# A row-wise skewness kernel: written instruction order, a new cut of the late units, one last DVE step, and load semaphores seen ahead of the store

## The chip, the cores and the metric

The kernel runs on one core of a Trainium2 chip. The metric is device time in microseconds (us) of the slowest core, here the only one; medians over several runs. The span in a profile is about 1.8 us shorter than the device time, since it runs from the first instruction to the last.

## The reference

```python
# x: 1024 x 8192 float32
mean = np.mean(x, axis=-1, keepdims=True)
std  = np.std(x, axis=-1, keepdims=True)
z = (x - mean) / (std + 1e-8)
return np.mean(z ** 3, axis=-1).astype(np.float32)
```

The kernel needs three sums per row, of x, of x squared and of x cubed, and a little arithmetic on them. The 1024 rows are eight blocks of 128, and one block is cut into units along its 8192 columns.

## The kernel before

For each unit: one load; a square with a row sum on ACT (ScalarE); a cube with a row sum on DVE (VectorE), which multiplies the square by x; and transposes on PE (TensorE), which add up the row sum of x in PSUM. At the end of a block ACT copies the transposed sums to SBUF and a matmul makes the mean. (SBUF and PSUM are the core's two on-chip memories.)

```python
UNITS = [
    [4096, 4096], [4096, 4096], [4096, 4096], [4096, 4096],
    [3584, 2304, 2304],
    [2304, 2304, 2048, 1536],
    [1664, 1792, 1920, 1664, 1152],
    [1024, 1024, 1152, 1280, 1408, 1152, 1152],
]
...
    for b, widths in enumerate(UNITS):
        for k, w in enumerate(widths):
            last_unit = b == L and k == len(widths) - 1
            nc.sync.dma_start(out=xt, in_=xv[b, :, c0 : c0 + w])
            for s, e in _slices(w):                  # at most 2304 columns each
                # sq: in SBUF; in PSUM for the last unit
                nc.scalar.activation(out=sq, in_=xt[:, s:e], func=AF.Square, scale=s_scale,
                                     accum_out=s2u[:, j : j + 1])
                nc.vector.scalar_tensor_tensor(out=cube, in0=sq, scalar=1.0, in1=xt[:, s:e],
                                     op0=ALU.mult, op1=ALU.mult, accum_out=s3u[:, j : j + 1])
            ...                                      # transposes of x, added up in tp
            if k > 0:
                next(pending, None); next(pending, None)   # steps of the block before
        nc.scalar.copy(out=tsb, in_=tp)
        nc.tensor.matmul(out=s1ps[:, b : b + 1], lhsT=tsb, rhs=onesn, start=True, stop=True)
        ...
    for _ in pending: pass                           # the last block's small ACT steps
    nc.gpsimd.tensor_tensor(out=rr, in0=var2, in1=expo[:, 0 : NB - F], op=ALU.pow)
    nc.vector.tensor_reduce(out=num, in_=..., axis=X_AXIS, op=ALU.add)
    nc.vector.tensor_tensor(out=skew[:, F:NB], in0=num, in1=rr, op=ALU.mult)
    nc.sync.dma_start(out=ov, in_=skew)
```

A scheduler puts the instructions of each engine in order. Eight unit buffers are in rotation, so SyncE issues a load when the unit eight before it has been used by ACT, PE and DVE.

Of the kernel before, what the change touches and what calls it, by code (L numbers as in the profile page):

```python
# [8 lines left out]
FP = mybir.dt.float32  # L9
AF = mybir.ActivationFunctionType  # L10
ALU = mybir.AluOpType
X_AXIS = mybir.AxisListType.X


UNITS = [
    [4096, 4096],
    [4096, 4096],
    [4096, 4096],
    [4096, 4096],
    [3584, 2304, 2304],  # L20
    [2304, 2304, 2048, 1536],
    [1664, 1792, 1920, 1664, 1152],
    [1024, 1024, 1152, 1280, 1408, 1152, 1152],
]
S1_ACT = {(0, 0): 1024, (1, 0): 1024, (2, 0): 1024}
SUB_MAX = 2304
X_BUFS = 8
SQ_BUFS = 4
EARLY = 6


def _slices(w):
    n = -(-w // SUB_MAX)
    step = -(-w // n // 128) * 128
    return [(s, min(s + step, w)) for s in range(0, w, step)]


@with_exitstack
def kernel(
    ctx: ExitStack,  # L40
    tc: tile.TileContext,
    x: bass.AP,
    out: bass.AP,
):
    nc = tc.nc
    P = nc.NUM_PARTITIONS
    R, C = x.shape
    NB = R // P
    L = NB - 1
    F = EARLY  # L50
    inv_n = 1.0 / float(C)
    s_scale = float(C) ** -0.5
    third = (1.0 / 3.0) ** 0.5
    assert len(UNITS) == NB and all(sum(u) == C for u in UNITS)
    nw = len(S1_ACT)
    assert sorted(b for b, _ in S1_ACT) == list(range(nw)) and nw <= F


    xv = x.rearrange("(p b) c -> b p c", b=NB)
    ov = out.rearrange("(p b) -> p b", b=NB)  # L60


    K = max(sum(len(_slices(w)) for w in u) for u in UNITS) + 1

    xpool = ctx.enter_context(tc.tile_pool(name="xp", bufs=X_BUFS))
    sqpool = ctx.enter_context(tc.tile_pool(name="sqp", bufs=SQ_BUFS))
    onep = ctx.enter_context(tc.tile_pool(name="onep", bufs=1))
    psum = ctx.enter_context(tc.tile_pool(name="ps", bufs=2, space=bass.MemoryType.PSUM))
    psum1 = ctx.enter_context(tc.tile_pool(name="ps1", bufs=1, space=bass.MemoryType.PSUM))

    def small(name, n):
        return onep.tile([P, n], FP, tag=name, name=name)

    onesn = small("onesn", 1)
    nc.vector.memset(onesn, inv_n)  # L75
    tiny = small("tiny", 1)
    nc.scalar.activation(out=tiny, in_=onesn, func=AF.Square)  # L77
    ident = small("ident", P)
    make_identity(nc, ident)
    s2u = small("s2u", NB * K)  # L80
    s3u = small("s3u", NB * K)
    nc.vector.memset(s2u, 0.0)
    nc.vector.memset(s3u, 0.0)
    s1a = small("s1a", nw)
    same = small("same", max(S1_ACT.values()))
    junk = small("junk", K)
    expo = small("expo", F)
    nc.gpsimd.memset(expo, -1.5)
    skew = small("skew", NB)
    s1ps = psum1.tile([P, NB], FP, tag="s1ps")  # L90
    m1a = small("m1a", F)
    var2 = small("var2", NB - F)
    Tsb = [small(f"tsb{i}", P) for i in range(2)]

    def close_first_blocks():

        m2, m3 = small("m2a", F), small("m3a", F)
        for dst, src in ((m2, s2u), (m3, s3u)):
            nc.vector.tensor_reduce(  # L99
                out=dst, in_=src[:, 0 : F * K].rearrange("p (b c) -> p b c", c=K),  # L100
                axis=X_AXIS, op=ALU.add,
            )
        m1sq, m1sq3, nm1 = small("m1sqa", F), small("m1sq3a", F), small("nm1a", F)
        nc.scalar.copy(out=m1a[:, nw:F], in_=s1ps[:, nw:F])
        nc.scalar.activation(out=m1sq, in_=m1a, func=AF.Square)
        nc.scalar.activation(out=m1sq3, in_=m1a, func=AF.Square, scale=third)
        nc.scalar.activation(out=nm1, in_=m1a, func=AF.Copy, scale=-3.0)
        g = nc.gpsimd
        var, rr = small("vara", F), small("rra", F)
        g.tensor_tensor(out=var, in0=m2, in1=m1sq, op=ALU.subtract)  # L110
        g.tensor_tensor(out=m1sq3, in0=m1sq3, in1=var, op=ALU.add)  # L111
        g.tensor_tensor(out=m1sq3, in0=m1sq3, in1=nm1, op=ALU.mult)  # L112
        g.tensor_tensor(out=m3, in0=m3, in1=m1sq3, op=ALU.add)  # L113
        g.tensor_tensor(out=rr, in0=var, in1=expo, op=ALU.pow)  # L114
        g.tensor_tensor(out=skew[:, 0:F], in0=m3, in1=rr, op=ALU.mult)  # L115

    def close_on_act(b):

        m2, m1sq, nm1, v3 = (small(f"{t}_{b}", 1) for t in ("m2", "m1sq", "nm1", "v3"))
        p1 = s1ps[:, b : b + 1]  # L120
        var = var2[:, b - F : b - F + 1]
        act = nc.scalar.activation
        yield act(out=junk, in_=s2u[:, b * K : b * K + K], func=AF.Copy, accum_out=m2)
        yield act(out=m1sq, in_=p1, func=AF.Square)  # L124
        yield act(out=var, in_=m1sq, func=AF.Identity, scale=-1.0, bias=m2)  # L125
        yield act(out=nm1, in_=p1, func=AF.Copy, scale=-3.0)  # L126
        yield act(out=v3, in_=m1sq, func=AF.Identity, scale=1.0 / 3.0, bias=var)  # L127
        yield act(  # L128
            out=s3u[:, b * K + K - 1 : b * K + K], in_=v3, func=AF.Identity, scale=nm1
        )  # L130

    pending = iter(())
    for b, widths in enumerate(UNITS):
        tp = psum.tile([P, P], FP, tag="tp", name=f"tp_{b}")
        c0 = 0
        j = b * K
        for k, w in enumerate(widths):
            last_unit = b == L and k == len(widths) - 1
            xt = xpool.tile([P, w], FP, tag="x", name=f"x_{b}_{k}")
            nc.sync.dma_start(out=xt, in_=xv[b, :, c0 : c0 + w])  # L140
            c0 += w
            for s, e in _slices(w):
                if last_unit:
                    sq = psum1.tile([P, e - s], FP, tag="sqps", name=f"sqps_{s}")
                else:
                    sq = sqpool.tile([P, e - s], FP, tag="sq", name=f"sq_{b}_{k}_{s}")
                nc.scalar.activation(  # L147
                    out=sq, in_=xt[:, s:e], func=AF.Square, scale=s_scale,
                    accum_out=s2u[:, j : j + 1],
                )  # L150
                cube = sqpool.tile([P, e - s], FP, tag="sq", name="cube") if last_unit else sq
                nc.vector.scalar_tensor_tensor(  # L152
                    out=cube, in0=sq, scalar=1.0, in1=xt[:, s:e],
                    op0=ALU.mult, op1=ALU.mult, accum_out=s3u[:, j : j + 1],
                )
                j += 1
            w_act = S1_ACT.get((b, k), 0)
            if w_act:
                nc.scalar.activation(  # L159
                    out=same[:, 0:w_act], in_=xt[:, w - w_act : w], func=AF.Copy,  # L160
                    scale=inv_n, accum_out=s1a[:, b : b + 1],
                )
            n = (w - w_act) // P
            for c in range(n):
                nc.tensor.matmul(  # L165
                    out=tp, lhsT=xt[:, c * P : (c + 1) * P], rhs=ident,
                    start=(k == 0 and c == 0), stop=(c0 == C and c == n - 1),
                    is_transpose=True,
                )
            if k > 0:  # L170
                next(pending, None)
                next(pending, None)
        tsb = Tsb[b % 2]
        nc.scalar.copy(out=tsb, in_=tp)  # L174
        nc.tensor.matmul(out=s1ps[:, b : b + 1], lhsT=tsb, rhs=onesn, start=True, stop=True)  # L175
        if b == F - 2:
            nc.vector.tensor_tensor(
                out=m1a[:, 0:nw], in0=s1ps[:, 0:nw], in1=s1a, op=ALU.add
            )
        if b == F - 1:  # L180
            close_first_blocks()
        if b >= F:
            pending = close_on_act(b)
    for _ in pending:
        pass
    rr = small("rr2", NB - F)
    nc.gpsimd.tensor_tensor(out=rr, in0=var2, in1=expo[:, 0 : NB - F], op=ALU.pow)  # L187
    num = small("num2", NB - F)
    nc.vector.tensor_reduce(  # L189
        out=num, in_=s3u[:, F * K :].rearrange("p (b c) -> p b c", c=K), axis=X_AXIS, op=ALU.add  # L190
    )
    nc.vector.tensor_tensor(out=skew[:, F:NB], in0=num, in1=rr, op=ALU.mult)  # L192
    nc.sync.dma_start(out=ov, in_=skew)


# [28 lines left out]
```

## Time and profile before

| | before |
|---|---|
| median, us | 91.64 (91.61 to 91.72, three runs) |
| span of the profile, us | 89.7 |
| last load landed, us from the span's start | 83.56 |
| last DVE step starts | 87.04 |
| store issued / landed | 87.23 / 88.65 |
| DMA busy, share of the span | 90% |

Read the table from the end: of 89.7 us, 83.6 are the stream of loads, 3.5 the arithmetic after it, 1.6 the way to the landed store, and 1.1 the closing of the program. The busy shares of the engines tell why only the tail can be changed:

```profile
PE 64.9 (72%) x504; PEld 59.3 (66%) x504; DVE 72.7 (81%) x80; ACT 72.1 (80%) x106; POOL 11.3 (13%) x14
```

No engine is near the 90% of the loads. The other lines are in the prediction.

### The profile page before, as it was taken

What the parts mean: (1) busy time and instruction counts of PE and PEld (TensorE: products, weight loads), DVE (VectorE), ACT (ScalarE), POOL (GpSimd) and SP (SyncE); (2) the same over time, 40 slices, a digit from 0 to 9 for tenths busy, and PEclk for the clock granted to TensorE, in tenths of its full rate; (3) what the DMA queues carried; (4) which work ended last, traced back from release to release, by engine and by line L of the source; (5) the groups of instructions that cost most, each with busy time, mean ns of one, the idle gap of its engine ahead of it and who ended that gap; (6) DMA issues with size and microseconds to landing.
All of it is one profiled execution on the core that took longest, in us unless ns stands there. A gap on an engine that the chain in (4) does not pass through costs nothing.

```text
span 89.7 us, 1368 instructions
## 1 busy us (share of the span) xinstructions
PE 64.9 (72%) x504; PEld 59.3 (66%) x504; DVE 72.7 (81%) x80; ACT 72.1 (80%) x106; POOL 11.3 (13%) x14
## 2 busy tenths in 40 slices
PE   0003999892882919989998988888987798969710
PEld 0003999791872909979897977877876787848500
DVE  1000498989999298995999999999999999999970
ACT  6003999699991999859898989978979898999950
POOL 3000000000000000000000000000005999900030
PEclk9999999999999997599999999999999999999998
DMA  3999999999999999999999999999999999994000
GB/s 117 351 424 438 424 431 431 431 431 424 446 416 431 424 438 424 424 438 427 415 409 418 419 427 419 421 415 419 409 414 417 404 413 411 421 412 161 0 0 2
DMA packets 4038, 33.64 MB, mean 375 GB/s; under 512 B 576, under 2 KB 576, under 8 KB 2240
## 3 DMA queue, kind: packets, MB, share of 16 engines
q1 hardware_dynamic: 4032, 33.56, 89.7%
q8 instruction: 4, 0.07, 0.3%
q14 instruction: 2, 0.02, 0.0%
HBM read 33.55 MB, written 0.00 MB: 374 GB/s over the span
## 4 chain that ended last, share of the span: by engine, by line
DMA 73%; ACT 13%; issue 5%; DVE 4%; SPq 1%; PE 1%; DVEq 0%; ACTq 0%
DMA x<-in_x_dram 73%; ACT sq L147 9%; DVE sq L152 3%; ACT sqps L147 1%; ACT same L159 1%; SPq L140 1%; PE s1ps L175 1%; ACT tsb L174 0%; ACT s3u L128 0%; ACT v L127 0%; ACT var L125 0%; DVE num L189 0%; ACT m1sq L124 0%; DVE skew L192 0%; ACT nm L126 0%
## 5 line engine op out<-in xcount | busy, mean ns | idle before, releaser
L152 DVE SCALAR_TENSOR_TENSOR sq<-sq,x 128x2048 f32<-128x2048 f32 (+9 forms) x35 | 70.7, 2071 | 13.4 <-ACT sq L147 13.3
L165 PE MATMUL tp<-ident,x 128*128 128x128 f32 x488 | 62.6, 288 | 17.3 <-DMA x<-in_x_dram 17.2
L165 PEld LDWEIGHTS tp<-ident,x 128*128 128x128 f32 x488 | 57.9, 150 | 20.9 <-DMA x<-in_x_dram 12.7
L147 ACT ACTIVATE sq<-x 128x2048 f32<-128x2048 f32 (+9 forms) x35 | 60.6, 1734 | 10.7 <-DMA x<-in_x_dram 9.9
L110 POOL TENSOR_TENSOR vara<-m2a,m1sqa 128x6 f32<-128x6 f32 x1 | 1.8, 1822 | 67.1 <-DVE m3a L99 67.1
L147 ACT ACTIVATION_READ_ACCUMULATOR sq<-x 128x1 f32 x35 | 6.5, 186 | 0.0
L175 PEld LDWEIGHTS s1ps<-onesn,tsb 128*128 128x128 f32 x16 | 2.4, 188 | 5.2 <-ACT tsb L174 5.2
L175 PE MATMUL s1ps<-onesn,tsb 128*128 128x1 f32 x16 | 3.1, 260 | 3.3 <-ACT tsb L174 3.3
L174 ACT COPY tsb<-tp 128x128 f32<-128x128 f32 x8 | 2.0, 256 | 2.0 <-PE tp L165 2.0
L114 POOL TENSOR_TENSOR rra<-vara,expo 128x6 f32<-128x6 f32 x1 | 3.3, 3267 | 0.0
L159 ACT ACTIVATE same<-x 128x1024 f32<-128x1024 f32 x3 | 3.1, 1041 | 0.0
L152 DVE DVE_READ_ACCUMULATOR sq<-sq,x 128x1 f32 x35 | 2.9, 83 | 0.0
L111 POOL TENSOR_TENSOR m1sq3a<-m1sq3a,vara 128x6 f32<-128x6 f32 x1 | 1.9, 1868 | 0.1
L77 ACT ACT_TABLE_LOAD x1 | 1.3, 1283 | 0.7 <-PEq L208 0.7
L187 POOL TENSOR_TENSOR rr<-var,expo 128x2 f32<-128x2 f32 x1 | 0.7, 702 | 7.7 <-ACT var L125 7.7
L152 DVE SCALAR_TENSOR_TENSOR cube<-sqps,x 128x1152 f32<-128x1152 f32 x1 | 1.4, 1350 | 0.0
L113 POOL TENSOR_TENSOR m3a<-m3a,m1sq3a 128x6 f32<-128x6 f32 x1 | 1.2, 1201 | 0.1
L147 ACT ACTIVATE sqps<-x 128x1152 f32<-128x1152 f32 x1 | 1.1, 1136 | 0.1
L115 POOL TENSOR_TENSOR skew<-m3a,rra 128x6 f32<-128x6 f32 x1 | 1.1, 1069 | 0.1
L124 ACT ACTIVATE m1sq<-s1ps 128x1 f32<-128x1 f32 x2 | 0.3, 171 | 0.5 <-PE s1ps L175 0.5
L75 DVE MEMSET onesn<- 128x1 f32 x1 | 0.1, 59 | 0.8 <-PEq L208 0.8
L112 POOL TENSOR_TENSOR m1sq3a<-m1sq3a,nm1a 128x6 f32<-128x6 f32 x1 | 0.7, 697 | 0.0
(28 smaller groups left out, 6.8 us busy)
## 6 DMA issues: line engine op xcount, KB each, us to landing
x<-in_x_dram SPq DMA_DIRECT2D x8, 2048.0 KB, 23.4
x<-in_x_dram SPq DMA_DIRECT2D x4, 1152.0 KB, 27.9
x<-in_x_dram SPq DMA_DIRECT2D x4, 576.0 KB, 8.6
x<-in_x_dram SPq DMA_DIRECT2D x1, 1792.0 KB, 33.0
x<-in_x_dram SPq DMA_DIRECT2D x2, 832.0 KB, 13.9
x<-in_x_dram SPq DMA_DIRECT2D x1, 1024.0 KB, 21.1
x<-in_x_dram SPq DMA_DIRECT2D x2, 512.0 KB, 10.0
x<-in_x_dram SPq DMA_DIRECT2D x1, 960.0 KB, 13.2
```

The lines of the kernel that those rows point to most:

```text
L77: nc.scalar.activation(out=tiny, in_=onesn, func=AF.Square)
L110: g.tensor_tensor(out=var, in0=m2, in1=m1sq, op=ALU.subtract)
L111: g.tensor_tensor(out=m1sq3, in0=m1sq3, in1=var, op=ALU.add)
L113: g.tensor_tensor(out=m3, in0=m3, in1=m1sq3, op=ALU.add)
L114: g.tensor_tensor(out=rr, in0=var, in1=expo, op=ALU.pow)
L115: g.tensor_tensor(out=skew[:, 0:F], in0=m3, in1=rr, op=ALU.mult)
L147: nc.scalar.activation(out=sq, in_=xt[:, s:e], func=AF.Square, scale=s_scale, accum_out=s2u[:, j : j + 1],)
L152: nc.vector.scalar_tensor_tensor(out=cube, in0=sq, scalar=1.0, in1=xt[:, s:e], op0=ALU.mult, op1=ALU.mult, accum_out=s3u[:, j : j + 1],)
L159: nc.scalar.activation(out=same[:, 0:w_act], in_=xt[:, w - w_act : w], func=AF.Copy, scale=inv_n, accum_out=s1a[:, b : b + 1],)
L165: nc.tensor.matmul(out=tp, lhsT=xt[:, c * P : (c + 1) * P], rhs=ident, start=(k == 0 and c == 0), stop=(c0 == C and c == n - 1), is_transp ...
L174: nc.scalar.copy(out=tsb, in_=tp)
L175: nc.tensor.matmul(out=s1ps[:, b : b + 1], lhsT=tsb, rhs=onesn, start=True, stop=True)
```

## The change

It intends to shorten what follows the last load: a narrower last unit, small steps moved out of the way, one DVE step at the end instead of two, and no waits behind the store that could be done ahead of it. These are waits for semaphores, the counters by which a load or an engine tells another that it is done; the last lines of the diff, called the early look below, make SyncE wait for the loads' semaphores before the store. The wide units of blocks 2 and 3 are also worked on in three slices instead of two. The diff, cut to its core:

```diff
-    [3584, 2304, 2304],
-    [2304, 2304, 2048, 1536],
-    [1664, 1792, 1920, 1664, 1152],
-    [1024, 1024, 1152, 1280, 1408, 1152, 1152],
+    [3072, 2944, 2176],
+    [2944, 2688, 2560],
+    [1664, 1536, 1664, 1792, 1536],
+    [1024, 1152, 768, 1024, 1024, 1280, 1024, 896],
...
+SUB_WIDE = 1408            # units of 3584 and more, from block 2 on, in three slices
...
+    ctx.enter_context(tc.manual_schedule(          # orders as written
+        engines={eng.PE, eng.Activation, eng.DVE, eng.Pool, eng.SP}))
...
+    for b in range(L):                             # copy and mean behind the next block's first unit
+        at(b + 1, 0, lambda b=b: copy_sums(b))
+        at(b + 1, 0, lambda b=b: mean(b))
...
+    at(L, 0, mid_sums)                             # block 6: two reductions on DVE,
+    at(L, 1, mid_power)                            # power on POOL,
+    at(L, 4, lambda: third_1(mid))                 # two small ACT steps
+    at(L, 5, lambda: third_2(mid))
...
-    nc.vector.tensor_reduce(out=num, in_=..., axis=X_AXIS, op=ALU.add)
-    nc.vector.tensor_tensor(out=skew[:, F:NB], in0=num, in1=rr, op=ALU.mult)
+    g.tensor_tensor(out=o["var"], in0=o["m2"], in1=o["m1sq"], op=ALU.subtract)
+    g.tensor_tensor(out=o["rr"], in0=o["var"], in1=expo[:, 0:1], op=ALU.pow)
+    act(out=o["nm1"], in_=p1, func=AF.Copy, scale=-3.0)
+    third_1(o)                                     # v3 = m2 - 2/3 m1sq
+    row_sum(o["m3"], s3u, n_sl[L] - 1)             # all cubes but the last
+    third_2(o)                                     # t = v3 * nm1 + m3
+    v.tensor_scalar(
+        out=skew[:, L:NB], in0=s3u[:, j - 1 : j], scalar1=o["t"], scalar2=o["rr"],
+        op0=ALU.add, op1=ALU.mult,
+    )
+    seen = nc.sync.nop()                           # SyncE sees all load semaphores here
+    for ld in loads[-8:]:
+        tc.add_manual_dep(seen.ins, ld.ins.name, SYNC_DEP)
     nc.sync.dma_start(out=ov, in_=skew)
```

More of the change, by code (lines that the diff above doesn't have):

```diff
@@ L11 @@
 ALU = mybir.AluOpType
+SYNC_DEP = mybir.DependencyInfo(
+    mybir.DependencyClass.Sync, mybir.DependencyReason.DATA
+)
 X_AXIS = mybir.AxisListType.X
@@ L26 @@
 SUB_MAX = 2304
+SUB_WIDE = 1408
+WIDE = 3584
 X_BUFS = 8
@@ L29, with _slices @@
 EARLY = 6
-def _slices(w):
-    n = -(-w // SUB_MAX)
+def _slices(b, w):
+    n = -(-w // (SUB_WIDE if b >= 2 and w >= WIDE else SUB_MAX))
     step = -(-w // n // 128) * 128
@@ L45 @@
     nc = tc.nc
+    eng = mybir.EngineType
+    ctx.enter_context(tc.manual_schedule(
+        engines={eng.PE, eng.Activation, eng.DVE, eng.Pool, eng.SP}))
     P = nc.NUM_PARTITIONS
@@ L53 @@
     third = (1.0 / 3.0) ** 0.5
-    assert len(UNITS) == NB and all(sum(u) == C for u in UNITS)
+    assert len(UNITS) == NB and all(sum(u) == C for u in UNITS) and F == L - 1
     nw = len(S1_ACT)
@@ L60 @@
     ov = out.rearrange("(p b) -> p b", b=NB)
-    K = max(sum(len(_slices(w)) for w in u) for u in UNITS) + 1
+    n_sl = [sum(len(_slices(b, w)) for w in u) for b, u in enumerate(UNITS)]
+    K = max(n_sl)
     xpool = ctx.enter_context(tc.tile_pool(name="xp", bufs=X_BUFS))
@@ L89, with at, copy_sums, mean @@
     skew = small("skew", NB)
-    s1ps = psum1.tile([P, NB], FP, tag="s1ps")
+    s1ps = psum1.tile([P, NB], FP, tag="s1ps", name="s1ps")
     m1a = small("m1a", F)
-    var2 = small("var2", NB - F)
     Tsb = [small(f"tsb{i}", P) for i in range(2)]
-    def close_first_blocks():
-        m2, m3 = small("m2a", F), small("m3a", F)
-        for dst, src in ((m2, s2u), (m3, s3u)):
-            nc.vector.tensor_reduce(
+    tps = {}
+    act, g, v = nc.scalar.activation, nc.gpsimd, nc.vector
+    loads = []
+    todo = {}
+    def at(b, k, fn):
+        todo.setdefault((b, k), []).append(fn)
+    def copy_sums(b):
+        nc.scalar.copy(out=Tsb[b % 2], in_=tps[b])
+    def mean(b):
+        nc.tensor.matmul(
+            out=s1ps[:, b : b + 1], lhsT=Tsb[b % 2], rhs=onesn, start=True, stop=True
+        )
+    for b in range(L):
+        at(b + 1, 0, lambda b=b: copy_sums(b))
+        at(b + 1, 0, lambda b=b: mean(b))
+    m2a, m3a, m1sqa, m1sq3a, nm1a, vara, rra = (
+        small(f"{t}a", F) for t in ("m2", "m3", "m1sq", "m1sq3", "nm1", "var", "rr")
+    )
+    def first_sums():
+        for dst, src in ((m2a, s2u), (m3a, s3u)):
+            v.tensor_reduce(
                 out=dst, in_=src[:, 0 : F * K].rearrange("p (b c) -> p b c", c=K),
@@ L102, in close_first_blocks @@
             )
-        m1sq, m1sq3, nm1 = small("m1sqa", F), small("m1sq3a", F), small("nm1a", F)
         nc.scalar.copy(out=m1a[:, nw:F], in_=s1ps[:, nw:F])
-        nc.scalar.activation(out=m1sq, in_=m1a, func=AF.Square)
-        nc.scalar.activation(out=m1sq3, in_=m1a, func=AF.Square, scale=third)
-        nc.scalar.activation(out=nm1, in_=m1a, func=AF.Copy, scale=-3.0)
-        g = nc.gpsimd
-        var, rr = small("vara", F), small("rra", F)
-        g.tensor_tensor(out=var, in0=m2, in1=m1sq, op=ALU.subtract)
@@ L111, in close_first_blocks @@
-        g.tensor_tensor(out=m1sq3, in0=m1sq3, in1=var, op=ALU.add)
-        g.tensor_tensor(out=m1sq3, in0=m1sq3, in1=nm1, op=ALU.mult)
-        g.tensor_tensor(out=m3, in0=m3, in1=m1sq3, op=ALU.add)
-        g.tensor_tensor(out=rr, in0=var, in1=expo, op=ALU.pow)
-        g.tensor_tensor(out=skew[:, 0:F], in0=m3, in1=rr, op=ALU.mult)
-    def close_on_act(b):
-        m2, m1sq, nm1, v3 = (small(f"{t}_{b}", 1) for t in ("m2", "m1sq", "nm1", "v3"))
-        p1 = s1ps[:, b : b + 1]
-        var = var2[:, b - F : b - F + 1]
-        act = nc.scalar.activation
-        yield act(out=junk, in_=s2u[:, b * K : b * K + K], func=AF.Copy, accum_out=m2)
-        yield act(out=m1sq, in_=p1, func=AF.Square)
-        yield act(out=var, in_=m1sq, func=AF.Identity, scale=-1.0, bias=m2)
-        yield act(out=nm1, in_=p1, func=AF.Copy, scale=-3.0)
-        yield act(out=v3, in_=m1sq, func=AF.Identity, scale=1.0 / 3.0, bias=var)
-        yield act(
-            out=s3u[:, b * K + K - 1 : b * K + K], in_=v3, func=AF.Identity, scale=nm1
-        )
@@ L132, with first_rest @@
-    pending = iter(())
+        act(out=m1sqa, in_=m1a, func=AF.Square)
+        g.tensor_tensor(out=vara, in0=m2a, in1=m1sqa, op=ALU.subtract)
+        g.tensor_tensor(out=rra, in0=vara, in1=expo, op=ALU.pow)
+    def first_rest():
+        act(out=m1sq3a, in_=m1a, func=AF.Square, scale=third)
+        act(out=nm1a, in_=m1a, func=AF.Copy, scale=-3.0)
+        g.tensor_tensor(out=m1sq3a, in0=m1sq3a, in1=vara, op=ALU.add)
+        g.tensor_tensor(out=m1sq3a, in0=m1sq3a, in1=nm1a, op=ALU.mult)
+        g.tensor_tensor(out=m3a, in0=m3a, in1=m1sq3a, op=ALU.add)
+        g.tensor_tensor(out=skew[:, 0:F], in0=m3a, in1=rra, op=ALU.mult)
@@ new lines, with mid_sums @@
+    at(F - 2, 0, lambda: v.tensor_tensor(
+        out=m1a[:, 0:nw], in0=s1ps[:, 0:nw], in1=s1a, op=ALU.add))
+    at(F, 1, first_sums)
+    at(F, 2, first_rest)
+    names = ("m2", "m3", "m1sq", "nm1", "var", "v3", "rr", "t")
+    mid, end = ({t: small(f"{t}_{b}", 1) for t in names} for b in (F, L))
+    def mid_sums():
+        for t, src in (("m2", s2u), ("m3", s3u)):
+            v.tensor_reduce(
+                out=mid[t], in_=src[:, F * K : F * K + n_sl[F]], axis=X_AXIS, op=ALU.add
+            )
@@ new lines, in mid_power, with third_1, third_2 @@
+    def mid_power():
+        act(out=mid["m1sq"], in_=s1ps[:, F : F + 1], func=AF.Square)
+        act(out=mid["nm1"], in_=s1ps[:, F : F + 1], func=AF.Copy, scale=-3.0)
+        g.tensor_tensor(out=mid["var"], in0=mid["m2"], in1=mid["m1sq"], op=ALU.subtract)
+        g.tensor_tensor(out=mid["rr"], in0=mid["var"], in1=expo[:, 0:1], op=ALU.pow)
+    def third_1(o):
+        act(out=o["v3"], in_=o["m1sq"], func=AF.Identity, scale=-2.0 / 3.0, bias=o["m2"])
+    def third_2(o):
+        act(out=o["t"], in_=o["v3"], func=AF.Identity, scale=o["nm1"], bias=o["m3"])
@@ L133 @@
+    at(L, 0, mid_sums)
+    at(L, 1, mid_power)
+    at(L, 4, lambda: third_1(mid))
+    at(L, 5, lambda: third_2(mid))
+    at(L, 5, lambda: g.tensor_tensor(
+        out=skew[:, F : F + 1], in0=mid["t"], in1=mid["rr"], op=ALU.mult))
     for b, widths in enumerate(UNITS):
-        tp = psum.tile([P, P], FP, tag="tp", name=f"tp_{b}")
+        tp = tps[b] = psum.tile([P, P], FP, tag="tp", name=f"tp_{b}")
         c0 = 0
@@ L139 @@
             xt = xpool.tile([P, w], FP, tag="x", name=f"x_{b}_{k}")
-            nc.sync.dma_start(out=xt, in_=xv[b, :, c0 : c0 + w])
+            loads.append(nc.sync.dma_start(out=xt, in_=xv[b, :, c0 : c0 + w]))
             c0 += w
-            for s, e in _slices(w):
+            for s, e in _slices(b, w):
                 if last_unit:
-                    sq = psum1.tile([P, e - s], FP, tag="sqps", name=f"sqps_{s}")
+                    sq = psum1.tile([P, e - s], FP, tag="sqps", name="sqps")
                 else:
                     sq = sqpool.tile([P, e - s], FP, tag="sq", name=f"sq_{b}_{k}_{s}")
-                nc.scalar.activation(
+                act(
                     out=sq, in_=xt[:, s:e], func=AF.Square, scale=s_scale,
@@ L151 @@
                 cube = sqpool.tile([P, e - s], FP, tag="sq", name="cube") if last_unit else sq
-                nc.vector.scalar_tensor_tensor(
+                v.scalar_tensor_tensor(
                     out=cube, in0=sq, scalar=1.0, in1=xt[:, s:e],
@@ L158 @@
             if w_act:
-                nc.scalar.activation(
+                act(
                     out=same[:, 0:w_act], in_=xt[:, w - w_act : w], func=AF.Copy,
@@ L169, with row_sum @@
                 )
-            if k > 0:
-                next(pending, None)
-                next(pending, None)
-        tsb = Tsb[b % 2]
-        nc.scalar.copy(out=tsb, in_=tp)
-        nc.tensor.matmul(out=s1ps[:, b : b + 1], lhsT=tsb, rhs=onesn, start=True, stop=True)
-        if b == F - 2:
-            nc.vector.tensor_tensor(
-                out=m1a[:, 0:nw], in0=s1ps[:, 0:nw], in1=s1a, op=ALU.add
-            )
-        if b == F - 1:
-            close_first_blocks()
-        if b >= F:
-            pending = close_on_act(b)
-    for _ in pending:
-        pass
-    rr = small("rr2", NB - F)
-    nc.gpsimd.tensor_tensor(out=rr, in0=var2, in1=expo[:, 0 : NB - F], op=ALU.pow)
-    num = small("num2", NB - F)
-    nc.vector.tensor_reduce(
-        out=num, in_=s3u[:, F * K :].rearrange("p (b c) -> p b c", c=K), axis=X_AXIS, op=ALU.add
-    )
-    nc.vector.tensor_tensor(out=skew[:, F:NB], in0=num, in1=rr, op=ALU.mult)
+            for fn in todo.pop((b, k), ()):
+                fn()
+    assert not todo
+    o, p1 = end, s1ps[:, L : L + 1]
+    def row_sum(out, src, n):
+        act(out=junk[:, 0:n], in_=src[:, L * K : L * K + n], func=AF.Copy, accum_out=out)
+    copy_sums(L)
+    row_sum(o["m2"], s2u, n_sl[L])
+    mean(L)
+    act(out=o["m1sq"], in_=p1, func=AF.Square)
+    g.tensor_tensor(out=o["var"], in0=o["m2"], in1=o["m1sq"], op=ALU.subtract)
[7 more added lines that the diff above has]
+        op0=ALU.add, op1=ALU.mult,
+    )
+    seen = nc.sync.nop()
+    for ld in loads[-8:]:
+        tc.add_manual_dep(seen.ins, ld.ins.name, SYNC_DEP)
     nc.sync.dma_start(out=ov, in_=skew)
```

## The prediction

> **What bounds the kernel now.** I read the page's rows of busy tenths first, then the chain that ended last, then the timeline of the last microseconds, then the waits of the DMA queue. The kernel reads 33.55 MB once, so the first question is whether the stream of loads ever pauses.
>
> ```profile
> DVE  1000498989999298995999999999999999999970
> DMA  3999999999999999999999999999999999994000
> DMA packets 4038, 33.64 MB, mean 375 GB/s; under 512 B 576, under 2 KB 576, under 8 KB 2240
> ```
>
> It does not: every slice from the second to the 36th is at nine tenths. DVE is full too from the middle on. The chain of work that ended last says where the one hands over to the other:
>
> ```profile
> 76.06 7.50 DMA x<-in_x_dram
> 83.56 0.02 issue
> 83.58 1.26 ACT sqps L147 x2
> 84.84 0.00 issue
> 84.84 0.28 ACT tsb L174
> 85.12 0.04 issue
> 85.16 0.40 PE s1ps L175 x2
> 85.56 0.02 issue
> 85.58 0.17 ACT m1sq L124
> ...
> 86.44 0.30 ACT s3u L128
> 86.74 0.02 issue
> 86.76 0.18 DVE num L189
> ...
> 87.04 0.16 DVE skew L192
> ```
>
> The last load lands at 83.56. Then come 3.48 us of tail before the last DVE step starts, and after it the store. The reader is to see that ACT, PE and two DVE steps in series make the tail, while POOL is not on it. The timeline of the tail shows what runs beside the chain (start, length, engine):
>
> ```profile
> 83.96 1.35 DVE L152 SCALAR_TENSOR_TENSOR sq<-sq,x 128x1152 f32<-128x1152 f32 x1
> ...
> 85.24 1.35 DVE L152 SCALAR_TENSOR_TENSOR cube<-sqps,x 128x1152 f32<-128x1152 f32 x1
> ...
> 86.16 0.70 POOL L187 TENSOR_TENSOR rr<-var,expo 128x2 f32<-128x2 f32 x1 [7.68 <-ACT var L125]
> ...
> 87.23 0.35 SPq L193 DMA_DIRECT2D out_dram<-skew  x1
> ```
>
> The last cube starts at 85.24 only because DVE is behind: ACT had the square at 84.72. It ends at 86.52 to 86.60, a mere 0.2 before the reduction that the chain names. So two paths end almost together. Last, the waits of the sync engine's queue:
>
> ```profile
> SPq L193 <- DVE skew L192: 10.8, 1, 10.8
> SPq L219 <- DMA out_dram<-skew: 1.1, 1, 1.1
> ```
>
> SyncE idles 10.8 us ahead of the store. In the trace's records of its instructions, five two-semaphore waits follow once the store has landed, starting at 88.665, 88.729, 88.791, 88.855 and 88.917, then a drain at 88.982, and the barrier among engines ends the span at 89.73.
>
> **What the Trainium skill says.** First, "DMA: Bandwidth & Descriptors", section "Specifications", gives 435 GB/s as the fabric ceiling. The trace agrees: wide units land 4.89 us apart (12.96, 17.85, 22.74 in the records of landings), 2.097 MB each, 429 GB/s. Second, "SBUF — State Buffer", section "Who interferes with whom": a DVE instruction with two SBUF inputs keeps out a GpSimd instruction that reads SBUF, and one with at most one SBUF input does not. The trace agrees in the middle: the POOL subtraction that starts at 68.38 ends at 70.20, 0.13 after the DVE cube of 68.26 gave way at 70.07; the next five end 0.13 or 0.14 after a cube too, except for the power of six columns, which ends 1.28 after a DVE gap (74.10). The last cube reads its square from PSUM, so the pow of two columns at 86.16 should have been free: 0.70. Third, "Perfetto Trace Analysis", section "GPSIMD Engine Instruction", calls reported POOL spans unreliable, so I give POOL wide margins. Fourth, the same page's section "Identifying Dependency Chains" says that waits on several engines may become separate EventSemaphore instructions ahead of the instruction; the five at 88.665 are of this kind.
>
> **The change part by part.** *Loads.* 27 loads before and after, the same bytes. Wide units land at 4.89 us per 4096 columns; 1152 columns took 1.37 to 1.44. Two points give about 1.18 ns a column and 0.06 us a load, so recutting the units leaves the sum alone. Could a load start late? The last one is issued when the unit eight before it is consumed. After the change that is the 1536-wide unit, landing about 10.1 us before the end (the eight later units are 8192 columns, 9.67 + 8 x 0.06). ACT and DVE need some 3.6 us for it, and the last load's turn on the engine that is furthest ahead comes 3.2 us before the end (its own 1.11 plus the 2.0 to 2.2 by which fast engines lead at each landing). With about 1.6 us of issue latency the margin is near 1.7 us. The end of the loads stays at 83.56, gain 0.
>
> *Slices and DVE backlog.* Starts of consecutive cubes give DVE's period: 2304 columns 2.48, 2048 2.21, 1664 1.81, 1152 1.28, 1024 1.14, that is 1.047 ns a column and 0.07 a cube. There are 36 cubes before and 44 after: 8 x 0.07 = 0.56 us more work. In return DVE gets its first slice of a wide unit 1.37 instead of 1.91 us after landing. Before, DVE never idles for long after 41.40. I check the sum on that: 40960 columns x 1.047 = 42.89, 24 cubes x 0.07 = 1.68, small reductions 0.30, together 86.27 against 86.52 seen: 0.25 of idle. After, the same count starts at the last wide unit: landing 43.53, first slice 1.37, hand-over 0.16, so 45.06. Then 36864 columns (38.60), 27 cubes (1.89), reductions 0.50: 86.05, and with the same 0.25 of idle 86.30. The backlog thus is the same and the gain is just the narrower last unit: 86.52 to 86.30, with its accumulator read 86.38.
>
> *ACT and PE of the last block.* The last unit is 896 wide instead of 1152. Its seven transposes take about 0.98 (nine took 1.20, thirteen 1.62: 0.107 each), its square 0.93 (1152: 1.14; 0.85 ns a column). The square begins a little late, at 83.65, because the small step for block 6 (0.19) stands before the square of the unit ahead. Copy at 84.60 instead of 84.84: 0.24 gained. The copy, the two matmul passes and the hand-overs to the mean's square keep their 0.74, so that square starts at 85.34 and is visible at 85.55. From there ACT needs the third (0.20 in pipeline), the row sum of the cubes (0.21 and 0.19 less 0.1 overlap), and the last product 0.29 with a hand-over: 86.40. The row sum needs the cube before last, which ends at about 85.3, in time.
>
> *POOL takes two steps onto the path.* Variance, then power, both 128x1. The subtraction can start at 85.55. The last cube runs from about 85.29 and has one SBUF input, so it should not block. I allow 0.3 for a subtraction (0.13 is seen after a release) and 0.55 for a power of one column (0.70 for two free, 1.28 for six after the gap), with 0.08 between: 86.50.
>
> *The last step.* DVE's single add-and-multiply waits for the latest of three: cube 86.38 + 0.1, ACT 86.40, POOL 86.50. With a hand-over it starts at about 86.55 instead of 87.04. The reduction (0.18) and its hand-over (0.1) are gone. Gain 0.49. Store and landing (88.665 - 87.04 = 1.62) are kept.
>
> *Semaphores seen early.* After the store SyncE has one two-semaphore wait and a drain instead of five and a drain; the built program shows it. Four x 0.063 = 0.25 gained. The five waits ahead of the store fall into SyncE's idle 10.8 us and cost nothing.
>
> Sum: 0 + 0.49 + 0.25 = 0.74. The copies moved behind the next block's first unit take away 2.0 us of ACT waits for PE (mostly 1.48 and 0.54, at 39 and 17 us), but the loads bound that stretch: nothing at the end.
>
> **The rivals.** *POOL becomes the bound.* If the cube does block it, the variance waits for 86.30, and the power ends near 86.30 + 0.13 + 0.08 + 0.35 = 86.86; the gain is then 0.1 + 0.25, time 91.3. For it: every POOL step in the middle of the trace did wait. Against: those cubes had two SBUF inputs. POOL's earlier chain for blocks 0 to 5 starts later too (about 71.4 instead of 68.4) and needs some 10 us, with three block 6 steps behind it, near 84.3: 1.2 us before its last pair is due. *DVE becomes the bound.* Eight cubes more and one more reduction leave the end where it was, or 0.5 later if a wait comes in: gain near 0.3, time 91.3 to 91.6. Against: first slices start sooner. *The loads move.* Four instruction fetches of 16 KB, about 1.05 us each, sit on single DMA engines (26.3, 47.4, 65.2, 80.9), and the first of them put the slowest engine 1.2 us back for good. Another arrangement of instructions could shift or add one: plus or minus up to 1 us, in which case 90.0 or 92. The PE stream that fills most of them has as many instructions as before, so I give it little. *Only the tail of semaphores pays.* Then 91.4.
>
> **Range and chances.** 91.64 - 0.74 = 90.90. POOL and DVE pull to 91.3, an unblocked and quicker POOL to 90.7. Eight in ten: 90.6 to 91.3. Faster by over 2% needs under 89.81, 1.83 us, over half of the whole 3.48 us tail: 0.03. Slower by over 2% needs 93.5, for which no mechanism is seen: 0.01. Within 2%: 0.96.
>
> **What would show it.** Right: the last load lands at 83.3 to 83.8; the last DVE step starts 3.0 us after it (2.8 to 3.2) instead of 3.48; one wait, not five, after the store lands, and 0.8 us from landing to the end instead of 1.06; the last cube starts within 0.2 of 85.29. Wrong: a power that ends 0.3 or more after the last cube (POOL blocked), a cube ending after 86.7 (DVE the bound), a last landing away from 83.56 by over 0.3 (the loads moved), or waits still standing behind the store. What would make it wrong altogether is a load held back by a buffer: a hole in the DMA row.

## The result, and the profile after

The changed kernel takes 91.2 us (91.12 to 91.26, six runs), the one before 91.62 in the same comparison. The ratio is 0.9955 (95% interval 0.9942 to 0.9968). Ratios here are the mean time of one kernel's runs over that of the other's of the same rounds, so they are not quite the ratio of the medians quoted. The gain is real, 0.42 us, but little more than half of the 0.74 expected.

The first view again, the rows of busy tenths, of the changed kernel:

```profile
DVE  1000498989989497999989999999999999999980
DMA  4899999999999999999999999999999999996000
DMA packets 4038, 33.64 MB, mean 376 GB/s; under 512 B 576, under 2 KB 576, under 8 KB 2240
```

The packets are the same in number and size, and there is no hole in the DMA row. The chain that ended last, from the third-last load's landing on (start, length, what):

```profile
73.55 7.78 DMA x<-in_x_dram
...
81.41 1.25 ACT sq L195
...
82.68 0.37 ACT t L172
83.05 1.04 ACT sq L195 x2
84.09 0.93 ACT sqps L195 x2
85.02 0.16 ACT tsb L112
...
86.37 0.40 ACT t L172
...
86.85 0.27 DVE skew L238
```

The reader is to compare where the loads end in this chain. Before, it ran from the last load straight to the last square. Now it leaves the loads two units earlier, at 81.33 (73.55 + 7.78), and from there ACT never pauses: square of unit 5 (counted from 0), the small step t of block 6 (third_2 in the code; third_1 is v), square of unit 6, last square. The last load landed at 83.66, but its square starts only at 84.00, 0.34 later instead of 0.02. ACT's serial work, not the last landing, now sets the tail; that is a reading of one chain, and the run with block 6's steps a unit earlier tests it.

Two shorter looks at the same timeline show POOL's part and the last step (start, length, engine):

```profile
85.89 0.19 POOL L232 TENSOR_TENSOR var<-m,m1sq 128x1 f32<-128x1 f32 x1 [1.47 <-ACT nm L234]
86.16 0.54 POOL L233 TENSOR_TENSOR rr<-var,expo 128x1 f32<-128x1 f32 x1
86.85 0.27 DVE L238 TENSOR_SCALAR skew<-s3u,t,rr 128x1 f32<-128x1 f32 x1 [0.31 <-ACT t L172]
87.15 0.35 SPq L246 DMA_DIRECT2D out_dram<-skew  x1
```

The subtraction runs in the middle of the last cube (85.44 to 86.54 with its accumulator read) and takes 0.19: it is not kept out. POOL is done at 86.70, ACT at 86.75; DVE waits 0.31 for them. And the one last step takes 0.27, where the last step of before took 0.16. At SyncE the records after the landed store are now one wait (88.590), a drain (88.655) and the barrier, which ends the span at 89.40: 0.83 us from landing to end instead of 1.08. The queue's waits show where the others went:

```profile
SPq L243 <- DMA x<-in_x_dram: 5.9, 3, 3.9
SPq L246 <- DVE skew L238: 3.4, 1, 3.4
SPq L272 <- DMA out_dram<-skew: 1.1, 1, 1.1
```

What was one wait of 10.8 us for the last DVE step is now 5.9 us for loads and 3.4 us for that step, so the early looks cost nothing.

The bill of the two profiles: last landing 0.10 later, from last landing to issue of the store 3.49 instead of 3.67, from landing of the store to the end 0.25 less; together 0.33 of span.

### The profile page after: what moved, and what is told of

Same layout as the page of the kernel before. It is cut to its first block, busy times and chain, and to the rows that moved or that the text cites. A ratio compares the mean times of both kernels' runs of the same rounds, so it can differ in the third digit from the quotient of the medians.

```text
span 89.4 us, 1405 instructions
## 1 busy us (share of the span) xinstructions
PE 62.8 (70%) x504; PEld 58.0 (65%) x504; DVE 73.5 (82%) x97; ACT 72.6 (81%) x120; POOL 13.7 (15%) x18
## 4 chain that ended last, share of the span: by engine, by line
DMA 58%; DVE 19%; ACT 14%; issue 5%; SPq 1%; PE 0%; ACTq 0%; DVEq 0%
DMA x<-in_x_dram 58%; DVE sq L200 18%; ACT sq L195 9%; ACT same L207 1%; ACT sqps L195 1%; SPq L188 1%; ACT t L172 1%; ACT tsb L112 0%; PE s1ps L115 0%; DVE skew L238 0%; ACT v L169 0%; ACT junk L226 0%; ACT m1sq L231 0%; DVE m2a L130 0%; DVE m3a L130 0%
## 5 line engine op out<-in xcount | busy, mean ns | idle before, releaser
L200 DVE SCALAR_TENSOR_TENSOR sq<-sq,x 128x1408 f32<-128x1408 f32 (+9 forms) x43 | 71.7, 1721 | 12.6 <-ACT sq L195 12.4
L195 ACT ACTIVATE sq<-x 128x1408 f32<-128x1408 f32 (+9 forms) x43 | 62.3, 1451 | 13.1 <-DMA x<-in_x_dram 12.4
L213 PE MATMUL tp<-ident,x 128*128 128x128 f32 x488 | 60.9, 284 | 15.2 <-DMA x<-in_x_dram 15.0
L213 PEld LDWEIGHTS tp<-ident,x 128*128 128x128 f32 x488 | 56.6, 148 | 18.2 <-DMA x<-in_x_dram 10.0
L195 ACT ACTIVATION_READ_ACCUMULATOR sq<-x 128x1 f32 x43 | 8.0, 187 | 0.0
L166 POOL TENSOR_TENSOR rr<-var,expo 128x1 f32<-128x1 f32 x1 | 1.4, 1426 | 0.1
L165 POOL TENSOR_TENSOR var<-m,m1sq 128x1 f32<-128x1 f32 x1 | 1.2, 1174 | 0.0
L200 DVE SCALAR_TENSOR_TENSOR cube<-sqps,x 128x896 f32<-128x896 f32 x1 | 1.1, 1089 | 0.0
L178 POOL TENSOR_TENSOR skew<-t,rr 128x1 f32<-128x1 f32 x1 | 1.0, 976 | 0.1
L195 ACT ACTIVATE sqps<-x 128x896 f32<-128x896 f32 x1 | 0.9, 897 | 0.0
```

What stands on the lines that cost most here:

```text
L166: g.tensor_tensor(out=mid["rr"], in0=mid["var"], in1=expo[:, 0:1], op=ALU.pow)
L195: act(out=sq, in_=xt[:, s:e], func=AF.Square, scale=s_scale, accum_out=s2u[:, j : j + 1],)
L200: v.scalar_tensor_tensor(out=cube, in0=sq, scalar=1.0, in1=xt[:, s:e], op0=ALU.mult, op1=ALU.mult, accum_out=s3u[:, j : j + 1],)
L213: nc.tensor.matmul(out=tp, lhsT=xt[:, c * P : (c + 1) * P], rhs=ident, start=(k == 0 and c == 0), stop=(c0 == C and c == n - 1), is_transp ...
```

## The experiments

Every kernel below gave a correct result. The first four and the last four ran on one chip and share their runs of the kernel before; the middle four ran on another. So compare ratios. Since the last landing moved between 83.53 and 83.83 from profile to profile, even between two profiles of the same kernel, I read the tail as times after the last landing:

| kernel | median | ratio, interval | last square starts | last cube starts | last DVE step starts | its length | store landed to end |
|---|---|---|---|---|---|---|---|
| before | 91.62 | 1 | 0.02 | 1.68 | 3.48 | 0.16 | 1.08 |
| changed | 91.20 | 0.9955, 0.9942 to 0.9968 | 0.34 | 1.78 | 3.19 | 0.27 | 0.83 |
| changed, early look out | 91.46 | 0.998, 0.9967 to 0.9994 | 0.34 | 1.76 | 3.20 | 0.27 | 1.07 |
| before with early look | 91.30 | 0.9966, 0.9953 to 0.998 | 0.02 | 1.67 | 3.48 | 0.16 | 0.83 |
| block 6's steps a unit earlier | 90.95 | 0.9929, 0.9916 to 0.9941 | 0.11 | 1.77 | 3.02 | 0.27 | 0.83 |
| one pointer in the last step | 91.12 | 0.9952, 0.9938 to 0.9965 | 0.33 | 1.76 | 3.20 | 0.22 | 0.83 |
| last square in SBUF | 91.64 | 0.9999, 0.9987 to 1.0011 | 0.34 | 1.77 | 3.57 | 0.27 | 0.83 |
| old cut | 91.33 | 0.9978, 0.9964 to 0.9991 | 0.26 | 1.61 | 3.33 | 0.27 | 0.83 |
| two slices | 91.22 | 0.9964, 0.9952 to 0.9977 | 0.34 | 2.04 | 3.28 | 0.27 | 0.83 |
| copies back | 91.17 | 0.9957, 0.9943 to 0.9971 | 0.33 | 1.83 | 3.18 | 0.27 | 0.83 |
| changed, again | 91.21 | 0.9954, 0.9939 to 0.9969 | 0.35 | 1.77 | 3.20 | 0.27 | 0.83 |
| both improvements | 90.90 | 0.9921, 0.9906 to 0.9937 | 0.10 | 1.77 | 3.02 | 0.22 | 0.83 |
| left to the scheduler | 91.45 | 0.9984, 0.9971 to 0.9996 | 0.56 | 2.21 | 3.45 | 0.27 | 0.83 |
| before, new cut and early look | 91.31 | 0.9961, 0.9945 to 0.9976 | 0.11 | 2.01 | 3.48 | 0.16 | 0.83 |

All the times after the last landing are from one profile of each kernel; the medians and ratios are from four to six runs of each, against six to eleven of the kernel before.

**The early look, taken out of the changed kernel.**

```diff
-    seen = nc.sync.nop()
-    for ld in loads[-8:]:
-        tc.add_manual_dep(seen.ins, ld.ins.name, SYNC_DEP)
```

> The changed kernel with its early look at the load semaphores taken out; all else the same. Theory (the four extra waits behind the store cost their 0.063 each on the path): five two-semaphore waits stand behind the landed store again, landing to end of span 1.06 instead of 0.81, time 0.25 more, near 91.45 (ratio to before 0.998). Rival (the early look pays nothing, the 0.4 come from the last DVE step): time unchanged at 91.2.

The five waits are back behind the store, at 88.710, 88.764, 88.825, 88.890 and 88.951 in SyncE's records (the first for one semaphore, the others for two), and landing to end is 1.07. Time 91.46, as the theory said.

**The early look alone, added to the kernel before.**

```diff
+    seen = nc.sync.nop()
+    for ld in loads[-8:]:
+        tc.add_manual_dep(seen.ins, ld.ins.name, SYNC_DEP)
     nc.sync.dma_start(out=ov, in_=skew)
```

> The kernel before with nothing but the early look added ahead of its store. Theory: 0.25 less, near 91.37 (ratio 0.997), the last DVE step still starting at 87.04 and the store issued at 87.23. Rival (the five waits ahead of the store delay it, as SyncE works through them only when it is due): store issued 0.3 later, time unchanged or worse.

The last DVE step starts at 87.04 and the store is issued at 87.23, to the hundredth as before; the span is 0.25 shorter. Time 91.30, ratio 0.9966. The rival falls. By the two ratios (0.998 - 0.9955 and 1 - 0.9966, times 91.6) these three lines are worth 0.23 to 0.31 of the whole 0.42.

**Block 6's two small ACT steps one unit earlier.**

```diff
-    at(L, 4, lambda: third_1(mid))
-    at(L, 5, lambda: third_2(mid))
+    at(L, 3, lambda: third_1(mid))
+    at(L, 4, lambda: third_2(mid))
```

> The changed kernel with block 6's two small ACT steps one unit earlier (after units 3 and 4 of the last block instead of 4 and 5), where ACT waits for loads anyway. Theory A (ACT's series of squares sets the tail: the step of 0.28 at 82.68 stands on it): last square starts at 83.72 instead of 84.00, copy of the sums at 84.70 instead of 84.93, ACT's and POOL's last results at 86.5; then DVE's own last cube at 86.54 is the latest and the last DVE step starts at 86.68 instead of 86.85: 0.17 less, near 91.03. Theory B (DVE's backlog alone sets the tail): the last DVE step starts at 86.85 as before, time 91.2.

In this kernel's timeline the same small step t stands before a wait for a load, and no longer between two squares:

```profile
80.76 0.37 ACT L172 ACTIVATE t<-v,m,nm 128x1 f32<-128x1 f32 x1
81.34 1.27 ACT L195 ACTIVATE sq<-x 128x1280 f32<-128x1280 f32 x1 [0.21 <-DMA x<-in_x_dram]
...
82.64 1.06 ACT L195 ACTIVATE sq<-x 128x1024 f32<-128x1024 f32 x1
...
83.69 0.90 ACT L195 ACTIVATE sqps<-x 128x896 f32<-128x896 f32 x1
...
84.65 0.27 ACT L112 COPY tsb<-tp 128x128 f32<-128x128 f32 x1
```

The 0.21 in brackets ahead of the square at 81.34 is idle time that is left over even so. The last square starts 0.11 after the last landing instead of 0.34, the last DVE step 3.02 after it instead of 3.19, and the time falls to 90.95. Theory A holds: DVE's last cube starts where it did (1.77 against 1.78), so it was not the cube that set the tail. Now it nearly is: its accumulator read ends at 86.45, ACT's t at 86.49, POOL's power at 86.44, all within 0.05.

**One pointer instead of two in the last step.**

```diff
-    v.tensor_scalar(
-        out=skew[:, L:NB], in0=s3u[:, j - 1 : j], scalar1=o["t"], scalar2=o["rr"],
+    v.scalar_tensor_tensor(
+        out=skew[:, L:NB], in0=s3u[:, j - 1 : j], scalar=o["t"], in1=o["rr"],
         op0=ALU.add, op1=ALU.mult,
     )
```

> The changed kernel with its last DVE step written with one per-partition scalar pointer and one tensor operand instead of two scalar pointers. Theory (the second pointer makes the step 0.27 long instead of the 0.16 that the last step took before): step 0.16 to 0.19, store issued about 0.1 earlier, time near 91.1. Rival (0.27 is the price of any last step that waits on three engines): unchanged, 91.2.

```profile
86.82 0.22 DVE L238 SCALAR_TENSOR_TENSOR skew<-s3u,t,rr 128x1 f32<-128x1 f32 x1 [0.34 <-ACT t L172]
```

The step takes 0.22, between 0.27 with two pointers and the 0.16 of a plain product with none (the last step of before). So the rival falls, since this step waits on the same three engines. I expected to win more. The rest of 0.06 I put down to the remaining pointer, but that is not separated: the three steps are three different instructions (TENSOR_SCALAR, SCALAR_TENSOR_TENSOR, TENSOR_TENSOR), and the product of before worked on two columns. The start, 3.20 after the last landing, has not moved. The ratio 0.9952 against 0.9954 and 0.9955 shows nothing in the time by itself; the profile alone shows the 0.05.

**The last square in SBUF instead of PSUM.**

```diff
-                if last_unit:
-                    sq = psum1.tile([P, e - s], FP, tag="sqps", name="sqps")
-                else:
+                if True:
                     sq = sqpool.tile([P, e - s], FP, tag="sq", name=f"sq_{b}_{k}_{s}")
```

> The changed kernel with the square of the last unit in SBUF instead of PSUM, so that the last cube has two SBUF inputs. Theory (POOL's variance is kept out while a cube reads two SBUF operands): the subtraction that took 0.19 from 85.89 ends only 0.13 after the last cube, near 86.6, the power near 87.1 to 87.2, the last DVE step starts at 87.2 to 87.3 instead of 86.85, time 91.55 to 91.65. Rival (the short POOL times at the end come from the narrow operands, not from PSUM): unchanged, 91.2.

POOL in this kernel's timeline:

```profile
85.81 0.67 POOL L230 TENSOR_TENSOR var<-m,m1sq 128x1 f32<-128x1 f32 x1 [1.49 <-ACT nm L232]
86.56 0.54 POOL L231 TENSOR_TENSOR rr<-var,expo 128x1 f32<-128x1 f32 x1
```

and DVE in the same:

```profile
85.34 1.09 DVE L198 SCALAR_TENSOR_TENSOR cube<-sq,x 128x896 f32<-128x896 f32 x1
86.35 0.08 DVE L198 DVE_READ_ACCUMULATOR cube<-sq,x 128x1 f32 x1
87.14 0.27 DVE L236 TENSOR_SCALAR skew<-s3u,t,rr 128x1 f32<-128x1 f32 x1 [0.70 <-POOL rr L231]
```

The same subtraction now takes 0.67 instead of 0.19 and ends at 86.48, 0.13 after the cube gave way at 86.35, and the last DVE step starts at 87.14, a little sooner than the 87.2 I had. DVE then waits 0.70 for the power. The whole gain is lost, 91.64. Two steps on POOL at the end are only affordable because the last cube has a single SBUF input; the rival I rated as "POOL becomes the bound" is what happens without that.

**The old cut of the late blocks.**

```diff
-    [3072, 2944, 2176], [2944, 2688, 2560],
-    [1664, 1536, 1664, 1792, 1536],
-    [1024, 1152, 768, 1024, 1024, 1280, 1024, 896],
+    [3584, 2304, 2304], [2304, 2304, 2048, 1536],
+    [1664, 1792, 1920, 1664, 1152],
+    [1024, 1024, 1152, 1280, 1408, 1152, 1152],
```

> The changed kernel with the old cut of blocks 4 to 7 (the last unit 1152 again). Theory (the loads end where they did, and the last cube ends later by the 256 columns): last landing 83.5 to 83.7, last square and transposes 0.2 longer, last cube ends 86.6 to 86.8, time 0.1 to 0.3 more, 91.3 to 91.5. Rival (the new cut only moves work about): within 0.05 of 91.2.

Last landing 83.66, the same as in the changed kernel's profile: recutting does not move the loads. The last DVE step starts 3.33 after it instead of 3.19; last cube done at 86.63, inside the range stated. Ratio 0.9978, 0.2 us more, with intervals that just overlap; the profile shows 0.13. The new cut is worth about 0.2 in this order, though not by its width alone: in the old cut "after unit 5" means straight ahead of the last unit, so that block 6's step t, 0.28 of ACT's time from 83.64, stands directly before the last square.

**Wide units of blocks 2 and 3 in two slices.**

```diff
-SUB_WIDE = 1408
+SUB_WIDE = 2304
```

> The changed kernel with the wide units of blocks 2 and 3 in two slices of 2048 again. Theory (DVE works without a pause from about 45 us, and what a slice saves at the head of a wide unit is 0.5 us of backlog less 0.07 for each cube): last cube ends 0.0 to 0.4 later, time 91.2 to 91.6. Rival (the slices of blocks 2 and 3 lie 40 us before the end and DVE's later waits swallow them): 91.2, the last cube starting at 85.44 as before.

The last cube starts 2.04 after the last landing instead of 1.78. So three slices, 40 us before the end, do save DVE 0.25 that is still there at the end: the rival (that later waits swallow it) falls. But the last DVE step starts only 0.09 later, because it waited for ACT anyway. The time, 0.9964 against 0.9955 and 0.9957 elsewhere, is within its interval; the loss in time is not settled.

**Copies at the end of their own block.**

```diff
-        at(b + 1, 0, lambda b=b: copy_sums(b))
-        at(b + 1, 0, lambda b=b: mean(b))
+        at(b, len(UNITS[b]) - 1, lambda b=b: copy_sums(b))
+        at(b, len(UNITS[b]) - 1, lambda b=b: mean(b))
```

> The changed kernel with the copy of the sums and the mean's matmul at the end of their own block again. Theory (the waits of ACT for PE that this brings back, 0.2 to 1.5 each, lie under the loads, but in blocks 5 and 6 they delay the first square of the next block and so DVE, which has no pause there): last cube ends 0 to 0.4 later, 91.2 to 91.6. Rival (nothing at the end depends on it): 91.2.

Nothing: 0.9957, last step 3.18. The rival holds. ACT's waits for PE came back (1.6 us in two waits) and lay under the loads.

**The control and the better version.** The changed kernel, unaltered, once more:

> The changed kernel once more, unaltered, as the control on the chip of this group. All theories: 0.9955 of before within 0.0015, last landing to last DVE step 3.19.

0.9954 and 3.20 after the last landing. Its last landing was at 83.83, against 83.66 in the first profile: that much of a profile's span is the loads' own scatter. With both improvements (the two diffs above together):

> The changed kernel with both improvements of the first group: block 6's small ACT steps one unit earlier and one pointer in the last DVE step. Theory (both lie on the same chain at its end, so they add): last landing to last DVE step 3.0, that step 0.22, time 0.3 less than the changed kernel, near 90.9, ratio to before 0.992. Rival (with ACT out of the way the DVE's own cube sets the end, and only one of the two counts): ratio 0.993 or more.

90.90, ratio 0.9921: 0.3 us better than the changed kernel and 0.7 better than before. The interval (0.9906 to 0.9937) lies clear of the changed kernel's 0.9954 and does not tell this kernel from the one with only the earlier steps (0.9929). In the profile they add: step 3.02 after the last landing, 0.22 long.

**The order left to the scheduler.**

```diff
-    ctx.enter_context(tc.manual_schedule(
-        engines={eng.PE, eng.Activation, eng.DVE, eng.Pool, eng.SP}))
```

> The changed kernel with its order left to the scheduler: the only undone part is 'orders as written'. The scheduler puts block 6's two small ACT steps after units 1 and 2 of the last block and the copies at the end of their own block. Theory (the written order lost 0.2 to 0.28 by the step at 82.68): last landing to last DVE step 3.0 to 3.05, time 90.95 to 91.05, faster than the changed kernel. Rival (the written order is worth something in the middle, where the scheduler lets ACT wait for PE): 91.3 or more.

My theory failed here. The scheduler does put block 6's small steps early, but too early: this is ACT's timeline at the start of the last block.

```profile
77.49 0.21 ACT L193 ACTIVATION_READ_ACCUMULATOR sq<-x 128x1 f32 x1
78.55 0.29 ACT L167 ACTIVATE v<-m1sq,m 128x1 f32<-128x1 f32 x1 [0.85 <-DVE m L156]
78.76 0.83 ACT L193 ACTIVATE sq<-x 128x768 f32<-128x768 f32 x1
...
79.58 0.37 ACT L170 ACTIVATE t<-v,m,nm 128x1 f32<-128x1 f32 x1
79.86 1.04 ACT L193 ACTIVATE sq<-x 128x1024 f32<-128x1024 f32 x1
```

The step v needs the sum that DVE forms behind the block's first cube, and DVE lags. ACT idles 0.85 us with a landed unit in its buffer. The square at 79.86 started at 78.54 in the changed kernel. ACT does not make it up: the last square starts 0.56 after the last landing and the last cube at 2.21. Time 91.45, 0.25 more. So the written order is worth that much, though not in the middle, as the rival had it (copies at the end of their own block cost nothing in the run above); with the steps a unit earlier it is worth about 0.5.

**The new cut and the early look in the kernel before.** The edit is the cut of the change and the early look as above, nothing else.

> The kernel before with the new cut of blocks 4 to 7 and the early look, and nothing else of the change. Theory (these two carry the whole gain, and orders, slices, copies and the rewritten tail together are worth nothing, since what they save is lost to the ACT step at 82.68 and the longer last DVE step): last landing to last DVE step 3.2 to 3.3, time 91.1 to 91.25, ratio to before 0.9945 to 0.996, not slower than the changed kernel by more than 0.05. Rival (the rewritten tail is needed for the narrow last unit to pay): 91.35 or more.

91.31, ratio 0.9961: by time it is not told from the changed kernel (0.9954) nor from the early look alone (0.9966). But the reason I gave is wrong. The last DVE step still starts 3.48 after the last landing, not 3.2 to 3.3: the last cube starts at 2.01 instead of 1.67. ACT is not the cause. Its last square starts 0.11 after the landing, and DVE's timeline shows no wait for it after the cube at 45.94; DVE is already late at the last block's first cube (77.54, against 77.16 in the changed kernel). This kernel cuts the wide units of blocks 2 and 3 into two slices, and the two-slice kernel above has its last cube at 2.04 as well. So the slices explain the delay by its size; a run of this kernel with three slices was not made. What the narrow last unit saves is lost to DVE's backlog. So the cut is worth about 0.2 in the changed kernel and nothing measurable without the rest of the change: the parts do not add.

## Why the prediction was right or wrong

The time lies within the range, and within 2% of before as forecast; the expected gain was nearly twice the real one. That the range still held it is partly luck: its upper side was meant for POOL or DVE, and neither used it. Point by point:

- *Loads, gain 0.* Right. Packets and bytes are the same, no hole, last landing 83.66 against 83.56. Other profiles show that this 0.10 is within the scatter (83.53 to 83.83 among eleven with the new cut). The 1.6 us of issue latency in that working is not read off a line; the store took 1.42 from issue to landing. The DMA row without a hole shows that the loads kept their margin.
- *Semaphores seen early, 0.25.* Right to the hundredth: landing to end 1.08 to 0.83. Shown from both sides, out of the changed kernel and into the one before.
- *Slices and DVE backlog.* Right in size. Last cube predicted at 85.29, 1.73 after the last landing; it started 1.78 after it. The two-slice kernel shows that the three slices are part of that.
- *POOL takes two steps onto the path.* Right in kind and size: 0.19 and 0.54 where I allowed 0.3 and 0.55, with the mechanism (one SBUF input in the last cube) shown by moving the square. (The "DVE gap" at 74.10 in the prediction is no gap: one cube hands over to the next there.) They started 0.34 later than I had them, 0.10 of it the later landing, the rest for ACT's reason. The rival's own sum was too kind, though: for a blocked POOL I counted 0.35 for the power, where I had 0.55 elsewhere. With 0.55 it ends at 87.06, and the last step gains nothing; the run with the last square in SBUF shows that case, with a power of 0.54 ending at 87.10 and the whole gain gone.
- *ACT and PE of the last block.* This is the step that was mis-sized. I let the last square begin at 83.65, 0.09 after the last landing; it began 0.34 after it, and everything behind it, copy, mean, POOL's pair and ACT's t, came that much later. The small step itself takes 0.28 of ACT's time, not 0.19, and it stands between two squares with no idle time to take it: unit 5's square ended at 82.66, when unit 6 had already landed (82.62). Moving it one unit ahead brings the last square to 0.11 and the last DVE step to 3.02 after the last landing, where I had predicted 2.99 with 86.55 - 83.56. That it comes so near is partly chance, since two more sizes were off and nearly cancel: POOL's pair takes 0.81 where I had 0.93, and the last block's own t takes 0.39 against the 0.29 I took from steps of before that carry one pointer fewer. The Trainium skill, "ScalarE: Activation LUTs", in section "What ACT_TABLE_LOAD costs", says that each per-partition pointer operand adds about 93 ns; the trace agrees (0.295 for v, 0.386 for t in the changed kernel), and I had not used it.
- *The last step, gain 0.49.* The start gained 0.28 (3.48 to 3.19) instead of 0.49, for the reason just told. Its length I kept at 0.16 without saying so; it is 0.27. Together the tail up to the store gained 0.17, which is 0.32 short, and with the 0.10 of landing this is the whole difference between the 0.74 of span that I expected and the 0.33 seen.
- *Rivals.* "POOL becomes the bound" was told apart by the SBUF square and did not happen. "DVE becomes the bound" did not either: DVE waited 0.31 for ACT. "Only the tail of semaphores pays" was nearer the truth than I rated it. None of the four named what happened, that ACT's own series of squares takes over from the last load.

Left open: why the last landing scatters by 0.3 from profile to profile, and whether three slices in blocks 2 and 3 pay in time at the end rather than only in DVE's start.

## What to carry to other kernels

When one engine takes nearly as long for a unit as the load of the next, a small step placed among the last units can be paid (here a step of 0.28 us put the last square 0.23 and the last DVE step 0.17 later, while the step v left an idle 0.26 behind it); place it where that engine still waits for loads, but not so early that it waits for another engine's result. Move final waits that are already met to a moment when their engine is idle, since each one left behind the last transfer is paid (here four waits, 0.25 us). A last step with fewer instructions is not the same as a short last step (here 0.27 instead of 0.16): look at its operands and its kind.

## What the Trainium skill lacked or had wrong

- "VectorE: DVE Perf Modes", section "Scalar operands", gives no cost for per-partition pointer scalars. As the last step, a product of two columns with none took 0.161 us, a one-column step with one 0.220, with two 0.273: some 0.055 each, if the kind of instruction and the second column cost nothing, which no run here separates.
- "SBUF — State Buffer", section "SBUF: two separate sides", says that whichever of the two starts first holds the shared pair for its whole instruction. The trace of before doesn't show it for POOL's side, as far as POOL's recorded spans can be trusted: its power of six columns, recorded from 72.11 and, by the page, kept out until the cube of 72.02 gave way at 74.10, ended at 75.38, in the middle of the next two-input cube (1664 columns, from 74.10), and that cube took 1.89 us, as the one at 68.26 took 1.88. So neither kept out the other there. The other side, a two-input cube that keeps POOL out until it ends, agrees: ends 0.13 to 0.14 after the cube.
- "Perfetto Trace Analysis", section "Identifying Dependency Chains", names the inserted EventSemaphore waits, not their price. Already met, they follow each other every 0.06 us on SyncE: four of them cost 0.25 us behind the last store and nothing ahead of it.
- "Perfetto Trace Analysis", section "GPSIMD Engine Instruction", calls reported POOL spans unreliable. For the two last steps here they were at least steady: 0.189 to 0.192 and 0.543 to 0.546 us over the ten profiles with the changed tail and its PSUM square. Where DVE waited for the power (the SBUF square), its step started 0.04 us after the recorded end, so that end was not far off.
